# An encoder layer on one core: the sample's squares, the gating by feature, and layer norm's end on other engines

## The chip, the core and the metric

The kernel runs on one core of a Trainium2 chip. The core has five engines that run side by side, each taking its own instructions strictly in their order: TensorE (PE in the profile; its weight loads are listed apart as PEld), VectorE (DVE), ScalarE (ACT), GpSimd (POOL) and SyncE (SP), which here issues most of the DMA transfers. They wait for one another through semaphores. Matmul results land in PSUM, of which the program uses eight banks of 128 x 512 fp32; everything else lives in SBUF with 128 partitions. The metric is the device time of one execution in microseconds (us).

## What is computed

A bidirectional encoder layer with a final norm, on two groups of tokens that share all weights: `prompt` (1024 tokens) and `sample` (256 tokens), 1024 features, fp32. Cut to what matters here:

```
h = rmsnorm(x, norm_mix_w)                 # mean of squares over the 1024 features
proj = h @ w_in                            # columns split into:
#   qkv (1536), ab (16), dn_gate (512), sg_u (512), sg_v (512), gate_a, gate_b (1024 each)
y_a = deltanet_branch(qkv, ab, dn_gate, ...) @ w_up_a
u = gelu(sg_u);  v = layernorm(gelu(sg_v), ln_w, ln_b)       # over 512 columns
mixed = einsum('gts,bnsgc->bntgc', w_s, v in chunks of 128 tokens) + b_s
y_b = (u * mixed) @ w_up_b
x = x + (sigmoid(gate_a) * y_a + sigmoid(gate_b) * y_b) @ w_out
x = x + memory_cross_attention(rmsnorm(x), rmsnorm(mem, norm_mem_w), ...)
x = x + swiglu(rmsnorm(x)) ;  y = rmsnorm(x, final_norm_w)
```

The deltanet branch is a gated delta rule in both directions. The change touches only the start: the norms of x and mem, and the gating columns `sg_v` with `ab`.

## The kernel before

Activations lie with features on the partitions: a tile `xs` or `x` is 8 feature blocks of 128 (k = 0 to 7) by tokens. Tokens come in three blocks, b = 0 (prompt, 512), b = 1 (prompt, 512) and b = 2 (sample, 256), and the work starts with b = 2, then 0, then 1. Every matmul is done to full precision with three matmuls of a faster format: each operand is split into a rounded part `hi` (ACT, L125) and a rest `lo` (DVE or POOL, L126), and PE adds hi by hi, lo by hi and hi by lo.

The first norm (`first_norm`, L379) squares `xs` on ACT, two features at a time (128 x 512), adds the four squares on DVE (`nacc`, L250), and lets PE sum over the partitions by a matmul of each 128-token slice with a column of ones (`one`, part of the constants `cst`). DVE takes the mean and a reciprocal root by ten small steps (`rsqrt`, L225 to L229, result `nst`), PE spreads it over the partitions (`bank<-cst,nst`), and then each feature is scaled (DVE, `nt`, L285) and split into `hi` and `lo`. The squares and the scaled features share three buffers (`nsq`, `nt`). The norms of x0, x1 (blocks 0 and 1) and mem (the memory tokens) run in `other_norms` (L395) beside other work, with one feature of 512 tokens in each addition.

The gating (`sgv`, L513) has tokens on the output partitions: for each chunk of 128 tokens (2 in b = 2, 4 in the others) and each half of the columns (264 and 248 plus 16 for `ab`), 24 matmuls of 264 columns, 3 for each feature. The weights are `svh` and `svl`. The result goes through a gelu (ACT square, DVE, ACT tanh, DVE: L426 to L429) into `vg`. Then `ln` (L445) takes the layer norm of `vg`: squares on ACT (`junk`), `rsqrt` on DVE (`sums`), and `vg = (vg - mu) * rs` on DVE (L458). Between the blocks come the projections `sgu(g, b)` (L561), 24 matmuls with `whi` and `wlo`, whose gelu writes `ug`; later `mix` (L544) multiplies `vg` with the spatial weights on PE (`bank<-sw,vg`) and adds to `ug`. `decays` (L463) turns `ab` into the decays (`gm`) of the delta rule by some thirty DVE steps.

PSUM is two pools of four banks: `pm` for the long sums (gating, projections), `pq` for the short ones. A bank is handed out in turn, so a new sum waits until the readout of the fourth before it has ended. PE's order is the order in which the program is written: the main line (gating, projections) calls the side jobs (norms, `ln`, `mix`) whenever a planned clock, advanced by each matmul, passes the time that the side job asked for with `yield`. The other engines' instructions are ordered beside this by the scheduler.

## Time and profile before

| | us |
|---|---|
| three runs: median (lowest to highest) | 2224.17 (2222.96 to 2227.03) |
| the profiled execution | 2224.42 |
| its span from first to last instruction | 2222.6 |
| PE busy | 2179.2 |
| DVE, ACT, POOL busy | 1391.3, 866.9, 555.3 |
| mean granted clock of TensorE | 0.997 |

PE is busy for 98% of the span. The timeline lists instructions with start and duration; behind them in brackets stands how long the engine had been idle and what ended that (`<-`). Matmuls are pipelined and their ends are modelled: the next starts before one ends, so the pace is the difference of two starts. A 128 x 1 matmul in fp32 appears as two passes, each with its own weight load.

### The profile page before, as it was taken

To read this page: it belongs to the slowest core of one execution; us is meant where nothing else is said; L and a number is where in the kernel's file an instruction comes from. 1 tells how busy PE (TensorE), PEld (TensorE's weight loads), DVE (VectorE), ACT (ScalarE), POOL (GpSimd) and SP (SyncE) were. 2 spreads that over 40 slices of the span, in tenths; PEclk is the share of its full clock that TensorE was granted. 3 is DMA by queue.
4 is the path that set the end of the run, shared out by engine and by line. 5 is a ranking of instruction groups with operands and counts; after the bars stand their busy time and mean duration, and the time that the engine had idled before them with its cause. 6 is when DMAs were issued, how large, how long until landed. Compare 5 with 4: busy or idle time off the path is not lost.

```text
span 2222.6 us, 32341 instructions
## 1 busy us (share of the span) xinstructions
PE 2179.2 (98%) x12416; PEld 1906.1 (86%) x12416; DVE 1391.3 (63%) x2657; ACT 866.9 (39%) x1625; POOL 555.3 (25%) x358
## 2 busy tenths in 40 slices
PE   6999999999999999999999999999999999999998
PEld 5988889898988899888888888888888888888888
DVE  7767777786974864687654546734443444378575
ACT  5434153443525443124544423422322232343453
POOL 3010000000000000034421332466666666200031
PEclk9999999999999999999999999999999999999999
DMA  5222332223234455971421441222222222493631
GB/s 181 82 82 74 100 77 89 75 72 97 74 112 127 154 148 167 332 236 39 166 86 57 158 152 57 95 86 82 87 81 76 78 86 90 141 347 127 204 109 58
DMA packets 192821, 263.52 MB, mean 119 GB/s; under 512 B 72394, under 2 KB 102682, under 8 KB 192666
## 3 DMA queue, kind: packets, MB, share of 16 engines
q1 hardware_dynamic: 172826, 232.34, 31.8%
q10 hardware_dynamic: 19840, 29.11, 3.6%
q8 instruction: 97, 1.59, 0.3%
q14 instruction: 58, 0.48, 0.1%
HBM read 183.24 MB, written 78.16 MB: 118 GB/s over the span
## 4 chain that ended last, share of the span: by engine, by line
PE 82%; DVE 6%; issue 5%; DMA 4%; ACT 1%; POOL 1%; SPq 0%; POOLq 0%; ACTq 0%; DVEq 0%
PE bank L108 81%; PE bank L121 1%; DMA tbd<-stage 1%; DMA braw<-gq 1%; DVE wlo L1232 0%; DVE xf L126 0%; DMA stage<-gtd 0%; DVE lo L126 0%; DVE x L1441 0%; DMA t<-sgd 0%; DMA gb<-tbd 0%; DMA r<-in_w_out 0%; DVE nacc L250 0%; DVE wlo L126 0%; DVE nt L285 0%
## 5 line engine op out<-in xcount | busy, mean ns | idle before, releaser
L108 PE MATMUL bank<-hi,whi 128*128 128x512 f32 (+1 forms) x1976 | 701.9, 355 | 0.0
L108 PE MATMUL bank<-hi,wlo 128*128 128x512 f32 (+1 forms) x1976 | 687.0, 348 | 0.0
L108 PE MATMUL bank<-lo,whi 128*128 128x512 f32 (+1 forms) x1976 | 686.8, 348 | 0.0
L108 PEld LDWEIGHTS bank<-hi,wlo 128*128 128x128 f32 x1976 | 373.6, 189 | 48.8
L108 PEld LDWEIGHTS bank<-hi,whi 128*128 128x128 f32 x1976 | 374.4, 189 | 43.8 <-issue 0.2
L108 PEld LDWEIGHTS bank<-lo,whi 128*128 128x128 f32 x1976 | 374.6, 190 | 43.4 <-issue 0.2
L125 ACT ACTIVATE whi<-raw 128x1024 fp32r<-128x1024 f32 (+1 forms) x136 | 137.0, 1010 | 258.3 <-PE bank L108 219.2
L126 POOL TENSOR_TENSOR wlo<-raw,whi 128x1024 fp32r<-128x1024 f32 x65 | 157.2, 2420 | 307.4 <-ACT whi L125 307.4
L108 PE MATMUL bank<-bhl,whi 128*128 128x512 f32 x408 | 125.9, 390 | 0.1
L126 DVE TENSOR_TENSOR wlo<-raw,whi 128x1024 fp32r<-128x1024 f32 (+1 forms) x71 | 81.7, 1151 | 66.0 <-ACT whi L125 65.6
L126 POOL TENSOR_TENSOR wlo<-x,whi 128x1024 fp32r<-128x1024 f32 x40 | 97.4, 2435 | 47.6 <-ACT whi L125 47.6
L2013 DVE TENSOR_TENSOR x<-x,bank 128x512 f32<-128x512 f32 x21 | 14.5, 688 | 125.5 <-ACT x L1808 125.5
L108 PEld LDWEIGHTS bank<-bhl,whi 128*128 128x128 f32 x408 | 76.5, 188 | 16.5 <-ACT whi L125 0.5
L615 DVE SCALAR_TENSOR_TENSOR acc<-craw,sm,acc 128x510 f32<-128x510 f32 (+1 forms) x96 | 72.9, 759 | 25.9 <-ACT acc L613 24.2
L1821 DVE SCALAR_TENSOR_TENSOR t<-t,x 128x512 f32<-128x512 f32 x42 | 64.2, 1530 | 28.4 <-ACT t L1820 28.4
L108 PE MATMUL bank<-bhl,wlo 128*128 128x512 f32 x204 | 79.7, 391 | 0.7 <-DVE wlo L126 0.5
L125 ACT ACTIVATE whi<-x 128x1024 fp32r<-128x1024 f32 (+1 forms) x48 | 49.0, 1025 | 79.9 <-PE bank L108 73.7
L250 DVE TENSOR_TENSOR nacc<-nacc,nsq 128x512 f32<-128x512 f32 (+1 forms) x68 | 58.0, 852 | 34.0 <-ACT nsq L249 32.8
L1830 DVE SCALAR_TENSOR_TENSOR t<-bank,t 128x512 f32<-128x512 f32 (+1 forms) x44 | 24.5, 558 | 82.5 <-PE bank L108 82.5
L108 PE MATMUL bank<-bhl,ahl 128*128 128x512 f32 x312 | 75.0, 395 | 0.0
L883 POOL COPY UT<-U 64x512 f32<-64x512 f32 x20 | 14.9, 752 | 238.8 <-PE bank L108 235.8
L982 ACT ACTIVATE gs<-bank 128x512 f32<-128x512 f32 (+1 forms) x60 | 31.1, 518 | 108.3 <-PE bank L108 102.9
(373 smaller groups left out, 4578.5 us busy)
## 6 DMA issues: line engine op xcount, KB each, us to landing
raw<-in_w_gu SPq DMA_DIRECT2D x44, 512.0 KB, 3.5
braw<-gq SPq DMA_DIRECT2D x14, 1024.0 KB, 7.2
raw<-in_w_g SPq DMA_DIRECT2D x20, 512.0 KB, 3.3
gq<-t SPq DMA_DIRECT2D x33, 256.0 KB, 2.0
gtd<-gs ACTq DMA_DIRECT2D x32, 256.0 KB, 2.2
w<-in_w_dn SPq DMA_DIRECT2D x8, 1024.0 KB, 12.4
raw<-in_w_qkv SPq DMA_DIRECT2D x12, 512.0 KB, 3.6
gq<-r SPq DMA_DIRECT2D x22, 256.0 KB, 2.1
```

The source lines that it names most:

```text
L108: self.nc.tensor.matmul(out, l, r, start=start, stop=stop, skip_group_check=more)
L121: self.nc.tensor.transpose(out, x, ident)
L125: self.last_hi = self.nc.scalar.activation(hi, src, AF.Copy).ins
L126: (eng or self.nc.vector).tensor_tensor(out=lo, in0=src, in1=f32(hi), op=ALU.subtract)
L250: (eng or V).tensor_tensor(out=self.acc, in0=self.acc, in1=sq, op=ALU.add)
L615: V.scalar_tensor_tensor(out=dst, in0=src, scalar=wj, in1=dst, op0=ALU.mult, op1=ALU.add)
L883: G.tensor_copy(Um[q, hs, :], U[d][q, hs, :])
L982: S.activation(t, ps, AF.Tanh, scale=0.5)
L1821: V.scalar_tensor_tensor(out=t, in0=t, scalar=1.0, in1=src, op0=ALU.add, op1=ALU.mult)
L1830: V.scalar_tensor_tensor(out=out, in0=u, scalar=sign, in1=t, op0=ALU.mult, op1=ALU.mult)
L2013: V.tensor_tensor(out=c22, in0=c22, in1=pe, op=ALU.add)
```

## The change

Four edits, all in the first 135 us or so of the program:

- The first norm's squares are no longer added on DVE. PE sums each of them with the column of ones as it comes (16 matmuls into 16 columns of one bank instead of 4 with accumulation), and DVE adds over the features with one reduction.
- The first half of the gating goes by feature instead of by chunk for b = 2 and b = 0: all chunks' banks are opened at once, and for each feature each chunk gets its three matmuls. In these blocks the second half takes its first two banks from the other pool.
- Layer norm's end moves from DVE to ACT, as `vg * rs + (-mu * rs)`, with one more small DVE step for the second term.
- The seven additions of squares of x1's and of mem's norm move from DVE to POOL, with later planned times for what follows them.

```diff
--- before.py
+++ after.py
@@ -300,10 +300,10 @@
         rsqrt(y, ms, sc)
         yield lag2
 
-    def norm(p, xk, n, wcol, sink, pace=1300, step=700, lag=1500):
+    def norm(p, xk, n, wcol, sink, pace=1300, step=700, lag=1500, eng=None):
         nm = Norm(p, n)
         for k in range(KT):
-            nm.add(xk(k))
+            nm.add(xk(k), eng)
             yield step
         yield from nm.rest(xk, wcol, sink, pace, lag=lag)
 
@@ -377,12 +377,28 @@
     x_h = act_tiles()
 
     def first_norm():
-
-        nm = Norm(xp, 512)
+        nm = Norm(xp, NS)
+        pc = bank()
         for k in range(0, KT, 2):
-            nm.add(xs[:, k : k + 2, :].rearrange("p k t -> p (k t)"))
-        nm.n = NS
-        yield from nm.rest(lambda k: xs[:, k, :], S_MIX, to_h(x_h, 2), 0, lag=0, halves=2)
+            sq = xp.tile([P, 512], F32, tag="nsq", name="nsq", bufs=3)
+            S.activation(sq, xs[:, k : k + 2, :].rearrange("p k t -> p (k t)"), AF.Square)
+            for i in range(2):
+                for c in range(2):
+                    mm(pc[:, 2 * (k + i) + c : 2 * (k + i) + c + 1], sq[:, i * NS + c * P : i * NS + c * P + P], one)
+        y = xp.tile([P, 4], F32, tag="nst", name="nst", bufs=2)[:, :2]
+        ms, sc = pc[:, 16:18], pc[:, 18:20]
+        V.tensor_reduce(out=ms, in_=pc[:, :16].rearrange("p (k c) -> p c k", c=2), axis=AX.X, op=ALU.add)
+        V.tensor_scalar(out=ms, in0=ms, scalar1=1.0 / D, scalar2=EPS, op0=ALU.mult, op1=ALU.add)
+        rsqrt(y, ms, sc)
+        pb = bank()
+        for c in range(2):
+            mm(pb[:, c * P : (c + 1) * P], y[:, c : c + 1].to_broadcast([P, P]), ident)
+        sink = to_h(x_h, 2)
+        for k in range(KT):
+            t = xp.tile([P, 512], F32, tag="nsq", name="nt", bufs=3)[:, :NS]
+            V.scalar_tensor_tensor(out=t, in0=xs[:, k, :], scalar=sm[:, S_MIX + k : S_MIX + k + 1], in1=pb[:, :NS], op0=ALU.mult, op1=ALU.mult)
+            sink(k, t)
+            yield 0
 
     first = K.side(first_norm())
     sv_split(0, sv_raw0)
@@ -397,11 +413,11 @@
         done.add(0)
         x1_ = x_load(a["xT"], 512, 512, "x1")
         yield 3000
-        yield from norm(xp, lambda k: x1_[:, k, :], 512, S_MIX, to_h(x_h, 1), 900)
+        yield from norm(xp, lambda k: x1_[:, k, :], 512, S_MIX, to_h(x_h, 1), 900, lag=3000, eng=G)
         done.add(1)
         mem = x_load(a["memT"], 0, 512, "mem")
         yield 6000
-        yield from norm(xp, lambda k: mem[:, k, :], 512, S_MEM, lambda k, t: SY.dma_start(md[k], t))
+        yield from norm(xp, lambda k: mem[:, k, :], 512, S_MEM, lambda k, t: SY.dma_start(md[k], t), step=1400, lag=4000, eng=G)
 
     norms = K.side(other_norms())
 
@@ -454,8 +470,9 @@
         V.tensor_scalar(out=var[:, cs], in0=var[:, cs], scalar1=1.0 / 512, scalar2=4.0 * EPS, op0=ALU.mult, op1=ALU.add)
         yield 2000
         rsqrt(rs[:, cs], var[:, cs], s0[:, cs])
+        V.scalar_tensor_tensor(out=mu[:, cs], in0=mu[:, cs], scalar=-1.0, in1=rs[:, cs], op0=ALU.mult, op1=ALU.mult)
         for c in range(cs.start, cs.stop):
-            V.tensor_scalar(out=vg[:, c, :], in0=vg[:, c, :], scalar1=mu[:, c : c + 1], scalar2=rs[:, c : c + 1], op0=ALU.subtract, op1=ALU.mult)
+            S.activation(vg[:, c, :], vg[:, c, :], AF.Identity, scale=rs[:, c : c + 1], bias=mu[:, c : c + 1])
 
     lns = {}
 
@@ -513,24 +530,37 @@
     def sgv(b):
         if b < 2:
             K.until(norms, lambda: b in done)
+        hi, lo = x_h[b]
+        chunks = [(c, slice((c % 4) * P, (c % 4 + 1) * P)) for c in range(4 * b, min(4 * b + 4, NCH))]
+
+        def part(ps, half, cs, k):
+            wh, wl = wk(sv[half], k, 264)
+            for n, (l, r) in enumerate(((hi[:, k, cs], wh), (lo[:, k, cs], wh), (hi[:, k, cs], wl))):
+                mm(ps[:, :264], l, r, k == 0 and n == 0, k == KT - 1 and n == 2)
+
+        def readout(ps, half, c):
+            nv = 264 if half == 0 else 248
+            acc = (s0 if half == 0 else s1)[:, c : c + 1]
+            gelu2(sp, ps[:, :nv], vg[:, c, half * 264 : half * 264 + nv], nv, acc)
+            if half:
+                V.tensor_copy(ab[:, c, :], ps[:, 248:264])
+
         for half in (0, 1):
-            w = sv[half]
-            nv = 264 if half == 0 else 248
-            for c in range(4 * b, min(4 * b + 4, NCH)):
-                cs = slice((c % 4) * P, (c % 4 + 1) * P)
-                hi, lo = x_h[b]
-                ps = bank(pm)
-                n = 0
+            if half == 0 and b != 1:
+                pss = [bank(pm) for _ in chunks]
                 for k in range(KT):
-                    wh, wl = wk(w, k, 264)
-                    for l, r in ((hi[:, k, cs], wh), (lo[:, k, cs], wh), (hi[:, k, cs], wl)):
-                        mm(ps[:, :264], l, r, n == 0, n == 23)
-                        n += 1
+                    for ps, (c, cs) in zip(pss, chunks):
+                        part(ps, 0, cs, k)
+                        yield 0
+                for ps, (c, cs) in zip(pss, chunks):
+                    readout(ps, 0, c)
+                continue
+            for i, (c, cs) in enumerate(chunks):
+                ps = bank() if half and b != 1 and i < 2 else bank(pm)
+                for k in range(KT):
+                    part(ps, half, cs, k)
                     yield 0
-                acc = (s0 if half == 0 else s1)[:, c : c + 1]
-                gelu2(sp, ps[:, :nv], vg[:, c, half * 264 : half * 264 + nv], nv, acc)
-                if half:
-                    V.tensor_copy(ab[:, c, :], ps[:, 248:264])
+                readout(ps, half, c)
         lns[b] = K.side(ln(slice(4 * b, min(4 * b + 4, NCH))))
         K.ahead()
```

The order moves at three places that matter here. Behind a row stands, in brackets, whose semaphores it waits for (`Activation` is ACT, `Pool` POOL, `DMAHW` a transfer). First, ACT's queue at the split of the weights of the gating's second half (`svh_119`; `hi2_101` are the sample's features, `nsq` the squares of `x0`). Before:

```order
L125 ACTIVATE hi2_101<-nt_183 128x256 [waits DVE_49]
L249 ACTIVATE nsq_218<-x0_109 128x512 [waits Pool_49]
L249 ACTIVATE nsq_221<-x0_109 128x512 [waits DMAHW2_49,DVE_49]
L249 ACTIVATE nsq_224<-x0_109 128x512 [waits DVE_49]
L249 ACTIVATE nsq_227<-x0_109 128x512 [waits DMAHW3_49,DVE_49]
L249 ACTIVATE nsq_230<-x0_109 128x512 [waits DVE_49]
L125 ACTIVATE svh_119<-raw_114 128x1056 [waits DMAHW5_49]
```

After:

```order
L125 ACTIVATE hi2_101<-nt_190 128x256 [waits DVE_49]
L249 ACTIVATE nsq_230<-x0_109 128x512 [waits DVE_49,PE_49,Pool_49]
L125 ACTIVATE hi2_101<-nt_194 128x256 [waits DVE_49]
L249 ACTIVATE nsq_233<-x0_109 128x512 [waits DMAHW2_49,Pool_49]
L249 ACTIVATE nsq_236<-x0_109 128x512 [waits DVE_49]
L249 ACTIVATE nsq_239<-x0_109 128x512 [waits DMAHW3_49,DVE_49]
L125 ACTIVATE svh_119<-raw_114 128x1056 [waits DMAHW5_49]
```

One square now stands in front of the last `hi2`, and three instead of five between it and `svh_119`.

Second, PE at the gating of b = 0, first half (`bank_519` is one chunk's bank; `bank_531` to `bank_534` are the four chunks' banks; `hi0`, `lo0` the features). Before:

```order
L108 MATMUL bank_519<-svh_104,hi0_97 128x264 [waits PE_49,Activation_49]
L108 MATMUL bank_519<-svh_104,lo0_98 128x264 [waits Pool_49]
L108 MATMUL bank_519<-svl_103,hi0_97 128x264
L108 MATMUL bank_519<-svh_104,hi0_97 128x264 [waits Activation_49]
L108 MATMUL bank_519<-svh_104,lo0_98 128x264 [waits DVE_49]
L108 MATMUL bank_519<-svl_103,hi0_97 128x264
L108 MATMUL bank_519<-svh_104,hi0_97 128x264 [waits Activation_49]
L108 MATMUL bank_519<-svh_104,lo0_98 128x264 [waits Pool_49]
L108 MATMUL bank_519<-svl_103,hi0_97 128x264
L108 MATMUL bank_519<-svh_104,hi0_97 128x264 [waits Activation_49]
```

After:

```order
L108 MATMUL bank_531<-svh_104,hi0_97 128x264 [waits Activation_49]
L108 MATMUL bank_531<-svh_104,lo0_98 128x264 [waits Pool_49]
L108 MATMUL bank_531<-svl_103,hi0_97 128x264
L108 MATMUL bank_532<-svh_104,hi0_97 128x264
L108 MATMUL bank_532<-svh_104,lo0_98 128x264
L108 MATMUL bank_532<-svl_103,hi0_97 128x264
L108 MATMUL bank_533<-svh_104,hi0_97 128x264 [waits DVE_49]
L108 MATMUL bank_533<-svh_104,lo0_98 128x264
L108 MATMUL bank_533<-svl_103,hi0_97 128x264
L108 MATMUL bank_534<-svh_104,hi0_97 128x264 [waits DVE_49]
L108 MATMUL bank_534<-svh_104,lo0_98 128x264
L108 MATMUL bank_534<-svl_103,hi0_97 128x264
```

and on DVE after, the last feature's `lo0` and the gelu of `sgu(1,2)`, which reads `bank_466`, the bank that `bank_534` takes over (`bank_533` takes over that of `sgu(0,2)`):

```order
L227 SCALAR_TENSOR_TENSOR sums_215<-sums_215 128x2 [waits DVE_49]
L443 SCALAR_TENSOR_TENSOR gt_521<-gt_521,bank_466 128x256
L228 TENSOR_TENSOR sums_215<-sums_215 128x2 [waits DVE_49]
L229 SCALAR_TENSOR_TENSOR sums_215<-sums_215 128x2 [waits DVE_49]
L126 TENSOR_TENSOR lo0_98<-nt_513,hi0_97 128x512 [waits Activation_49]
L227 SCALAR_TENSOR_TENSOR sums_215<-sums_215 128x2 [waits DVE_49]
L445 SCALAR_TENSOR_TENSOR ug_520<-gt_521,bank_466 128x256 [waits Activation_49]
```

The first chunk went through all features before the next began; now the third and fourth chunk of the first feature wait for DVE, and PE has no further wait for a `lo0` that DVE writes.

Third, ACT around the squares of mem and, now, layer norm's end for b = 0 (`vg_214`; `gt` are the gelu steps). Before:

```order
L246 ACTIVATE nacc_941<-mem_873 128x512 [waits DMAHW5_49]
L249 ACTIVATE nsq_949<-mem_873 128x512 [waits Pool_49]
L428 ACTIVATE gt_917<-gt_917 128x512 [waits DVE_49]
L249 ACTIVATE nsq_968<-mem_873 128x512 [waits DMAHW6_49,Pool_49]
L249 ACTIVATE nsq_980<-mem_873 128x512
L249 ACTIVATE nsq_998<-mem_873 128x512 [waits DMAHW7_49,DVE_49]
L249 ACTIVATE nsq_1016<-mem_873 128x512 [waits DVE_49]
L426 ACTIVATE gt_953<-bank_922 128x512 [waits PE_49]
L249 ACTIVATE nsq_1028<-mem_873 128x512 [waits DMAHW0_49,DVE_49]
L249 ACTIVATE nsq_1046<-mem_873 128x512 [waits DVE_49]
L428 ACTIVATE gt_953<-gt_953 128x512 [waits DVE_49]
```

After:

```order
L246 ACTIVATE nacc_970<-mem_906 128x512 [waits DMAHW5_49]
L249 ACTIVATE nsq_987<-mem_906 128x512 [waits Pool_49]
L444 ACTIVATE gt_930<-gt_930 128x512 [waits DVE_49]
L249 ACTIVATE nsq_1005<-mem_906 128x512 [waits DMAHW6_49,Pool_49]
L249 ACTIVATE nsq_1029<-mem_906 128x512
L442 ACTIVATE gt_961<-bank_935 128x512 [waits PE_49,Activation_49]
L475 ACTIVATE vg_214<-vg_214,sums_215 128x512 [waits DVE_49]
L475 ACTIVATE vg_214<-vg_214,sums_215 128x512 x2
L475 ACTIVATE vg_214<-vg_214,sums_215 128x512 [waits Activation_49]
L444 ACTIVATE gt_961<-gt_961 128x512 [waits DVE_49]
L249 ACTIVATE nsq_1053<-mem_906 128x512 [waits DMAHW7_49,Pool_49]
```

The last passes over `vg` now stand in this queue, with mem's `nsq_1053` and a tanh behind them, and the squares wait for POOL where they waited for DVE.

## Prediction

> **What bounds the kernel now.** I read the page first, then busy time by stretch, then the instruction timeline of each engine over the first 135 us, since the order of the two programs differs nowhere behind that on the engines that TensorE (PE) waits for. The page says which engine is full, and the stretches say where it isn't (columns of the second view: stretch, its length, then busy us and instructions of PE, PEld, DVE, ACT and POOL, the granted clock, DMA share and GB/s).

> ```profile
> span 2222.6 us, 32341 instructions
> PE 2179.2 (98%) x12416; PEld 1906.1 (86%) x12416; DVE 1391.3 (63%) x2657; ACT 866.9 (39%) x1625; POOL 555.3 (25%) x358
> ```

> ```profile
> 0.00:20.00 20.00, 7.13 (x27) 6.14 (x28) 10.06 (x27) 9.31 (x16) 5.12 (x9) 1.00 0.88 311
> 20.00:52.00 32.00, 25.63 (x174) 23.22 (x174) 27.82 (x68) 18.57 (x37) 14.10 (x8) 0.94 0.25 75
> 52.00:102.00 50.00, 50.00 (x362) 47.88 (x361) 39.95 (x119) 27.28 (x58) 5.53 (x4) 0.97 0.27 98
> 102.00:135.00 33.00, 31.25 (x200) 27.73 (x199) 26.51 (x80) 12.08 (x28) 4.96 (x2) 1.00 0.27 98
> 135.00:2222.00 2087.00, 2065.15 (x11661) 1801.11 (x11659) 1286.92 (x2365) 799.65 (x1488) 525.55 (x336) 1.00 0.36 118
> ```

> PE is the bound. Of its 43.4 idle us, 12.9 lie in the first 20, 6.4 from 20 to 52, none from 52 to 102 and 1.8 up to 135. Behind 135 all keeps its order, so the change is worth what it does to PE's arrival there. So a gain has at most 21 us to come from, and much of that is the loading of the inputs.

> **1. Sample's squares on TensorE.** The timeline of the first norm (start, duration, engine, line, output and inputs, idle time before it and what ended it):

> ```profile
> 2.75 0.47 SPq L373 DMA_DIRECT2D sm<-in_small  x1
> 3.26 0.43 SPq L374 DMA_DIRECT2D cst<-in_const  x1
> 7.37 0.17 DVE L421 TENSOR_SCALAR h<-sm 128x9 f32<-128x9 f32 x1 [1.75 <-DMA sm<-in_small]
> 7.46 1.49 DVE L250 TENSOR_TENSOR nacc<-nacc,nsq 128x512 f32<-128x512 f32 x2
> 9.00 1.78 PEld L108 LDWEIGHTS bank<-cst,nacc 128*128 128x128 f32 x8 [9.00 <-DVE nacc L250]
> 9.00 1.87 PE L108 MATMUL bank<-cst,nacc 128*128 128x1 f32 x8 [9.00 <-DVE nacc L250]
> 13.11 1.22 PE L108 MATMUL bank<-cst,nst 128*128 128x128 f32 x4 [2.24 <-DVE nst L229]
> 31.61 0.95 PE L108 MATMUL bank<-cst,nacc 128*128 128x1 f32 x8
> ```

> The three additions on DVE go (they end at 8.95). In their place stand 16 column sums instead of 4. In the trace four such instructions are eight passes, 1.78/8 = 0.22 us each at 9.00; the same eight take 0.95 us at 31.61, where PE has warmed up. The sums need the column of ones. Its load is issued behind `sm`, and `sm` is awaited until 7.37, so PE starts no sooner than about 7.5, whenever the squares are there. 32 passes at 0.22 end at 7.5 + 7.1 + 0.1 = 14.7, where DVE took the result at 10.9 before: 3.8 later. The added reduction over features I put at 0.2, by the small DVE instruction at 7.37 (0.17). Together **+4.0**. At the warm price (0.12 a pass) the same sum is 7.5 + 3.8 + 0.2 = 11.5, +0.6. I take the cold one: it is the same work at the same place, and there PE had idled before it as it will again. DVE's rsqrt, PE's spread at 13.11 and the eight features only move along. The fourth square now waits for PE to free a buffer (9.4 instead of 6.5). Behind it on ACT stands the split of the gating weights; PE needs these with the first feature, which is itself 4 us later, so this costs nothing.

> [...]

> **2. What the second half of the gating waits for.** This norm is not what PE waits for longest:

> ```profile
> 20.44 2.82 ACT L249 ACTIVATE nsq<-x 128x512 f32<-128x512 f32 x5 [0.18 <-POOL lo L126]
> 23.17 1.07 ACT L125 ACTIVATE svh<-raw 128x1056 fp32r<-128x1056 f32 x1
> 24.31 2.94 POOL L126 TENSOR_TENSOR svl<-raw,svh 128x1056 fp32r<-128x1056 f32 x1 [3.90 <-ACT svh L125]
> 24.87 0.28 PE L108 MATMUL bank<-svh,lo 128*128 128x264 f32 x1
> 27.31 0.40 PE L108 MATMUL bank<-svl,hi 128*128 128x264 f32 x1 [2.17 <-POOL svl L126]
> ```

> PE finishes the sample's first half just before 24.87 and then waits 2.17 for `svl`, that is for ACT, which squared five features of x0 ahead of `svh`. So a faster first half is worth nothing here: by feature, PE does both chunks while the features come, and waits longer at the same place. Cost and gain of that edit at b = 2: 0, covered by this wait. What moves is ACT's queue. Three squares now stand between the last `hi` and `svh`, and one has slipped in front of the last `hi`. One square less is 2.82/5 = 0.56; at best the two that are gone and the pause after the last `hi` count in full, 1.4. I take **-1.1**. It goes against the +4.0, because all eight `hi` stand ahead of `svh`: PE starts the second half 2.9 later than at 27.31, and x0's norm behind it as well.

> **3. By feature at b = 0.** Here the four chunks open four banks at once, and the pool has four. Two of them are still held by the projections `sgu(0,2)` and `sgu(1,2)`, and the order shows PE waiting for DVE at the third and fourth chunk of the first feature, with DVE's release of the last one behind all eight `lo`.

> ```profile
> 50.57 0.69 DVE L126 TENSOR_TENSOR lo<-nt,hi 128x512 fp32r<-128x512 f32 x1
> 51.25 0.41 DVE L429 SCALAR_TENSOR_TENSOR ug<-gt,bank 128x256 f32<-128x256 f32 x1
> 44.09 0.29 PE L108 MATMUL bank<-svh,hi 128*128 128x264 f32 x1
> 51.32 0.49 PE L108 MATMUL bank<-svh,lo 128*128 128x264 f32 x1 [0.34 <-DVE lo L126]
> 54.24 0.42 PE L108 MATMUL bank<-svl,hi 128*128 128x264 f32 x1
> 54.46 0.42 PE L108 MATMUL bank<-svh,hi 128*128 128x264 f32 x1
> 62.83 0.28 PE L108 MATMUL bank<-svh,hi 128*128 128x264 f32 x1
> 62.95 0.28 PE L108 MATMUL bank<-svh,lo 128*128 128x264 f32 x1
> ```

> The last `lo` is the first row, the release (the write of `ug`) the second: 51.66. Before, PE had by then done the whole first chunk, 24 of 96 matmuls, between the features. Now it has done 9 of them, from 44.09 on, and has 87 left instead of 72 or 73: 14.5 more at 0.12 (62.83 to 62.95), **+1.75**. The slow stretch remains: after 51.32 matmuls follow at 0.22 (54.24 to 54.46), and PE will have been idler still. One slow stretch of this length more or less is 1.6 us, so this term lies between +0.1 and +3.4. Using the other pool for two chunks of the second half hides the four readouts that now come together: PE has two chunks, 5.8 us, before it needs a bank of theirs.

> **4. x1's and mem's sums on GpSimd, layer norm's end on ScalarE.** Rows from the groups (the POOL row) and from the timeline:

> ```profile
> L250 POOL TENSOR_TENSOR nacc<-nacc,nsq 128x512 f32<-128x512 f32 x14 | 22.3, 1595 | 164.6 <-ACT nsq L249 163.7
> 84.83 2.34 ACT L249 ACTIVATE nsq<-mem 128x512 f32<-128x512 f32 x4
> 88.69 1.92 DVE L458 TENSOR_SCALAR vg<-vg,sums 128x512 f32<-128x512 f32 x4
> 89.71 1.44 PE L108 MATMUL bank<-sw,vg 128*128 128x128 f32 x8
> 121.70 2.43 POOL L126 TENSOR_TENSOR wlo<-raw,whi 128x1024 fp32r<-128x1024 f32 x1 [42.08 <-ACT whi L125]
> 121.80 2.35 DVE L228 TENSOR_TENSOR sums<-sums 128x4 f32<-128x4 f32 x1
> 127.06 3.95 DVE L458 TENSOR_SCALAR vg<-vg,sums 128x512 f32<-128x512 f32 x4
> ```

> POOL does such an addition in 1.6 us, so each norm's seven take 11.2. For x1 that is hidden: they run beside the 87 matmuls, and PE asks for the sum 30 matmuls after those. For mem the seven additions are done long before PE asks, too. But ACT's squares of mem, POOL's additions and the small DVE steps of layer norm's rsqrt for b = 0 now meet in one place, and PE stands behind them: the mix `sw,vg` at 89.71. Before, `vg` was ready from 88.69 on, in 1.92 us, and PE hardly waited. Now x1's spread stands 13 matmuls later, so its features and with them layer norm's squares come 13 x 0.12 = 1.6 later. Four additions of mem that stood among DVE's steps are off DVE, which is worth up to 2.8 and, as DVE paused among them, about 1.9. One step more is added (0.2), and four passes on ACT take 2.34 (four squares of the same size) instead of 1.92. Undisturbed: 1.6 - 1.9 + 0.2 + 0.4 = +0.3.

> The disturbance is the pair at 121.7: a DVE step on 4 columns took 2.35 because POOL was at work. Three additions can meet DVE's steps (the fourth square waits behind `vg` on ACT). None gives +0.3, all three 0.3 + 4.8 = 5.1. I take one, 0.3 + 1.6 = **+1.9**. Behind `vg` on ACT wait the tanh of the open readout and mem's later squares, for which PE has slack.

> **5. The same for b = 1.**

> ```profile
> 104.38 2.06 DVE L285 SCALAR_TENSOR_TENSOR nt<-mem,sm,bank 128x512 f32<-128x512 f32 x3 [0.46 <-issue]
> 125.44 0.44 DVE L497 SCALAR_TENSOR_TENSOR gm<-wk,rows 128x32 f32<-128x32 f32 x4
> 127.78 0.63 PE L108 MATMUL bank<-cst,gm 128*40 128x128 f32 x4
> ```

> mem's spread comes some 70 matmuls later, so five of its eight passes (2.06/3 = 0.69 each, 3.4 in all) now stand between the last readout and the decays `gm`. PE took `gm` 1.9 after DVE had it, so 1.5 of this shows. Against it, `vg` leaves DVE, where it took 3.95 beside POOL: on ACT 2.34, 1.6 less. Net **0**, from -1.6 (the passes find room) to +3 (POOL's weight splits hit the decays).

> Sum: 4.0 - 1.1 + 1.75 + 1.9 + 0 = +6.6. The profiled execution took 2224.42 for its span of 2222.6; its own time plus 6.6 is **2231.0**. The median of the runs shown, 2224.17, is 0.25 lower, well inside their spread of 4.

> **The rivals.** [...]

> *By feature pays at b = 0* (not slower). If the banks were free in time, before PE reaches the third chunk six matmuls after 44.09, all 96 matmuls would run from 44.09 without a gap: 11.5 + 0.75 for the mixes between, done at 56.4 instead of 62.83. That is -6.5 in place of +1.75, in all 2222.8, or 2218 with the better ends of the other terms. It decides at the release of `ug`: before about 45 it pays, and in the trace the last came at 51.66. Against it stands the order on DVE; I see nothing for it but the possibility that I misread which bank is reused.

> *GpSimd's additions meet everything.* All three at b = 0 (+3.2 on my term) and the weight splits at b = 1 (+3): 2237. For it stand the rows at 121.7 and 127.06.

> **How the numbers follow.** Forecast 0.48 (2231, own range 2226 to 2235), warm sums 0.25 (2228.4), by feature 0.15 (2222.8), additions meet everything 0.12 (2237). A measurement of this kernel tells about 0.2% (4.4 us) from no change, so faster is below 2219.8, slower above 2228.6. Slower: 0.36 of the forecast's 0.48, 0.12 of the second, all 0.12 of the last: 0.60. Faster: 0.08 of the third, 0.02 of the first and 0.01 of the second: 0.11. The rest, 0.29, is the same. The range 2220 to 2237 leaves out about 0.1 below and 0.07 above.

> **What would show it.** Right: the rsqrt of the first norm starts on DVE near 15, the second half of the gating near 30; at b = 0 PE makes nine matmuls on the first feature, with two waits on `ug`, and stands until some 54; the first mix of b = 0 has a wait of about 2 us on ACT. Wrong: the first column sum before 7.3 or passes at 0.12 from the start; no wait on `ug`; DVE's small steps at 0.2 while GpSimd adds. If PE is at 135 us' place within 4 us of before, terms 3 and 4 were too dear.

## Result and the profile after

The changed kernel takes 2238.45 us (median of four runs, 2237.0 to 2241.14) against 2223.57 (2222.61 to 2227.03) for the kernel before on the same chip: a ratio of 1.0067, 95% interval 1.0055 to 1.008. It is slower by about 15 us; the forecast was slower by 6.6. The direction held and most of the waits stand where they were expected; the size did not hold, and one term of the sum, the decays of b = 1, was reckoned wrongly. The traced execution of the changed kernel is the fastest of its four, at 2237.0.

The page after, first lines, and busy time by stretch (columns as in the prediction):

```profile
span 2235.2 us, 32397 instructions
PE 2188.2 (98%) x12440; PEld 1916.3 (86%) x12440; DVE 1377.9 (62%) x2634; ACT 873.5 (39%) x1635; POOL 574.5 (26%) x372
```

```profile
0.00:20.00 20.00, 9.13 (x38) 8.47 (x39) 5.41 (x19) 7.57 (x11) 3.71 (x7) 1.00 0.82 278
20.00:52.00 32.00, 24.27 (x170) 22.36 (x169) 28.62 (x69) 19.98 (x41) 15.26 (x10) 0.98 0.27 92
52.00:102.00 50.00, 45.33 (x294) 42.39 (x295) 30.37 (x85) 28.51 (x59) 19.62 (x16) 0.91 0.26 90
102.00:135.00 33.00, 33.00 (x235) 31.16 (x234) 20.73 (x72) 11.47 (x29) 6.37 (x4) 1.00 0.23 84
135.00:160.00 25.00, 21.43 (x97) 17.60 (x96) 13.12 (x35) 7.54 (x12) 2.34 (x1) 0.80 0.19 66
```

The last stretch in the kernel before:

```profile
135.00:160.00 25.00, 25.00 (x139) 21.70 (x138) 10.91 (x19) 5.61 (x10) 2.52 (x5) 1.00 0.20 72
```

Before, PE was never idle from 52 to 102; now it stands 4.7 us there, and 3.6 us more from 135 to 160. In both stretches the granted clock is down as well (0.91 and 0.80). These two columns together are most of the result: PE waits, and then works at half speed. The 1.00 of the first stretch is no proof of a full clock: the first clock record of this trace comes at 23.67 us, and the column reads 1.00 ahead of it. What shows the half clock there is the pace, 0.22 us a pass.

How late PE is can be read from one and the same matmul in both timelines. Its start before and after, and what was lost since the row above:

| matmul | before | after | late | lost here |
|---|---|---|---|---|
| spread of the first norm | 13.11 | 16.58 | +3.47 | +3.5 |
| second half of b = 2, first with `svl` | 27.31 | 29.17 | +1.86 | -1.6 |
| first of the gating of b = 0 | 44.09 | 45.32 | +1.23 | -0.6 |
| first of `sgu(0,0)`, behind it | 76.29 | 80.66 | +4.37 | +3.1 |
| first of `sgu(0,1)`, behind the gating of b = 1 | 115.01 | 124.27 | +9.26 | +4.9 |
| behind the third mix of b = 0 | 147.97 | 163.34 | +15.37 | +6.1 |
| 2207 us, near the end | | | +12.86 | -2.5 |

PE's timeline after, at these places:

```profile
7.17 6.96 PE L108 MATMUL bank<-cst,nsq 128*128 128x1 f32 x32 [7.17 <-DMA cst<-in_const]
16.58 1.22 PE L108 MATMUL bank<-cst,nst 128*128 128x128 f32 x4 [2.46 <-DVE nst L229]
29.17 0.39 PE L108 MATMUL bank<-svl,hi 128*128 128x264 f32 x1 [1.53 <-POOL svl L126]
48.80 0.39 PE L108 MATMUL bank<-svh,hi 128*128 128x264 f32 x1 [2.59 <-DVE ug L445]
53.00 0.59 PE L108 MATMUL bank<-svh,hi 128*128 128x264 f32 x1 [3.57 <-DVE ug L445]
80.66 0.40 PE L108 MATMUL bank<-hi,whi 128*128 128x512 f32 x1
97.15 0.49 PE L108 MATMUL bank<-sw,vg 128*128 128x128 f32 x2 [2.91 <-ACT vg L475]
97.85 0.49 PE L108 MATMUL bank<-sw,vg 128*128 128x128 f32 x2 [0.22 <-ACT vg L475]
98.56 1.50 PE L108 MATMUL bank<-sw,vg 128*128 128x128 f32 x4 [0.22 <-ACT vg L475]
139.87 1.08 PE L108 MATMUL bank<-cst,gm 128*40 128x128 f32 x4 [2.76 <-DVE gm L514]
141.76 2.91 PE L108 MATMUL bank<-sw,vg 128*128 128x128 f32 x8 [0.81 <-ACT vg L475]
```

The waits are where the prediction put them: two on `ug`, one on `vg`, one on the decays `gm`. Behind the long ones stands a stretch at half clock. The first mix of b = 1 is no measure of it: its passes come two by two, 0.70 us apart, which is the pace at which ACT writes `vg`, and they do so in e5 below as well, where the clock is 1.00. The granted clock behind the wait on `vg` and behind that on `gm`, of the kernel after:

```profile
97.00:103.00 6.00, 5.35 (x26) 4.68 (x27) 2.47 (x4) 5.44 (x11) 2.42 (x2) 0.72 0.00 1
139.00:150.00 11.00, 9.32 (x30) 7.28 (x31) 5.58 (x18) 4.25 (x7) 0.62 (x1) 0.53 0.22 75
```

0.72 over 6 us is one stretch of some 3.4 us at half, 0.53 over 11 us is nearly all of it.

What the waits at b = 0 and b = 1 come from stands on DVE (one ACT row among them): the small steps of the layer norm of b = 0 that met GpSimd's additions, `vg`, and at b = 1 the first and last of mem's five late passes, two small steps that met GpSimd's weight split, and the decays.

```profile
91.93 1.21 DVE L228 TENSOR_TENSOR sums<-sums 128x4 f32<-128x4 f32 x1
93.37 1.14 DVE L227 SCALAR_TENSOR_TENSOR sums<-sums 128x4 f32<-128x4 f32 x1
95.03 0.82 DVE L228 TENSOR_TENSOR sums<-sums 128x4 f32<-128x4 f32 x1
96.28 2.93 ACT L475 ACTIVATE vg<-vg,sums 128x512 f32<-128x512 f32 x4 [2.49 <-DVE sums L473]
126.25 0.73 DVE L285 SCALAR_TENSOR_TENSOR nt<-mem,sm,bank 128x512 f32<-128x512 f32 x1
...
130.57 0.74 DVE L285 SCALAR_TENSOR_TENSOR nt<-mem,sm,bank 128x512 f32<-128x512 f32 x1
131.22 2.35 DVE L504 TENSOR_TENSOR wk<-wk 128x80 f32<-128x80 f32 x1
...
137.32 2.32 DVE L228 TENSOR_TENSOR sums<-sums 128x4 f32<-128x4 f32 x1
139.56 0.43 DVE L514 SCALAR_TENSOR_TENSOR gm<-wk,rows 128x32 f32<-128x32 f32 x4
```

From the last `ab` copy to `gm` DVE took 8.4 us before (117.08 to 125.44) and takes 13.2 now (126.33 to 139.56).

### The profile page after: what moved, and what is told of

Read it like the earlier page. It is cut to its first block, busy times and chain, and to the rows that moved or that the text cites. A ratio compares the mean times of both kernels' runs of the same rounds, so it can differ in the third digit from the quotient of the medians.

```text
span 2235.2 us, 32397 instructions
## 1 busy us (share of the span) xinstructions
PE 2188.2 (98%) x12440; PEld 1916.3 (86%) x12440; DVE 1377.9 (62%) x2634; ACT 873.5 (39%) x1635; POOL 574.5 (26%) x372
## 4 chain that ended last, share of the span: by engine, by line
PE 82%; DVE 7%; issue 4%; DMA 4%; ACT 2%; POOL 1%; SPq 0%; POOLq 0%; DVEq 0%; ACTq 0%
PE bank L108 81%; DMA tbd<-stage 1%; PE bank L121 1%; DVE xf L126 1%; DMA braw<-gq 1%; DVE x L1471 1%; DVE nt L285 1%; DMA t<-sgd 1%; DVE wlo L1262 1%; DVE lo L126 0%; DMA stage<-gtd 0%; DVE wlo L126 0%; DMA gb<-grd 0%; DMA raw<-in_w_u 0%; POOL nacc L250 0%
## 5 line engine op out<-in xcount | busy, mean ns | idle before, releaser
L108 PE MATMUL bank<-hi,whi 128*128 128x512 f32 (+1 forms) x1976 | 703.4, 356 | 0.0
L108 PE MATMUL bank<-hi,wlo 128*128 128x512 f32 (+1 forms) x1976 | 688.2, 348 | 0.3 <-POOL wlo L126 0.3
L108 PE MATMUL bank<-lo,whi 128*128 128x512 f32 (+1 forms) x1976 | 688.0, 348 | 0.0
L108 PEld LDWEIGHTS bank<-hi,wlo 128*128 128x128 f32 x1976 | 374.4, 189 | 49.5 <-POOL wlo L126 0.5
L108 PEld LDWEIGHTS bank<-hi,whi 128*128 128x128 f32 x1976 | 375.5, 190 | 44.1 <-issue 0.2
L108 PEld LDWEIGHTS bank<-lo,whi 128*128 128x128 f32 x1976 | 375.7, 190 | 43.7 <-issue 0.2
L125 ACT ACTIVATE whi<-raw 128x1024 fp32r<-128x1024 f32 (+1 forms) x136 | 137.0, 1010 | 257.3 <-PE bank L108 218.1
L126 POOL TENSOR_TENSOR wlo<-raw,whi 128x1024 fp32r<-128x1024 f32 x65 | 157.7, 2428 | 295.7 <-ACT whi L125 295.7
L108 PE MATMUL bank<-bhl,whi 128*128 128x512 f32 x408 | 125.9, 390 | 0.0
L126 DVE TENSOR_TENSOR wlo<-raw,whi 128x1024 fp32r<-128x1024 f32 (+1 forms) x71 | 81.6, 1150 | 66.6 <-ACT whi L125 66.4
L126 POOL TENSOR_TENSOR wlo<-x,whi 128x1024 fp32r<-128x1024 f32 x40 | 97.5, 2437 | 46.9 <-ACT whi L125 46.8
L108 PEld LDWEIGHTS bank<-bhl,whi 128*128 128x128 f32 x408 | 76.4, 188 | 16.5 <-ACT whi L125 0.5
L250 POOL TENSOR_TENSOR nacc<-nacc,nsq 128x512 f32<-128x512 f32 x28 | 40.7, 1455 | 180.9 <-ACT nsq L249 179.2
L125 ACT ACTIVATE whi<-x 128x1024 fp32r<-128x1024 f32 (+1 forms) x48 | 49.0, 1025 | 79.9 <-PE bank L108 73.7
L108 PE MATMUL bank<-bhl,wlo 128*128 128x512 f32 x204 | 79.6, 390 | 0.5 <-DVE wlo L126 0.5
L913 POOL COPY UT<-U 64x512 f32<-64x512 f32 x20 | 14.9, 752 | 238.0 <-PE bank L108 235.0
L108 PE MATMUL bank<-bhl,ahl 128*128 128x512 f32 x312 | 75.0, 395 | 0.0
```

The lines of the kernel that those rows point to most:

```text
L108: self.nc.tensor.matmul(out, l, r, start=start, stop=stop, skip_group_check=more)
L125: self.last_hi = self.nc.scalar.activation(hi, src, AF.Copy).ins
L126: (eng or self.nc.vector).tensor_tensor(out=lo, in0=src, in1=f32(hi), op=ALU.subtract)
L250: (eng or V).tensor_tensor(out=self.acc, in0=self.acc, in1=sq, op=ALU.add)
L913: G.tensor_copy(Um[q, hs, :], U[d][q, hs, :])
```

## Experiments

e1 to e10 take the change apart; v1 and v2 try to make the kernel before faster. "Late" is, as above, how much later than in the trace of before PE starts the same matmul; these differences come from one profiled execution of each kernel, and between two executions they scatter by a microsecond or two. The last column is the difference of the medians, each against runs of the kernel before that were timed beside it. These were four groups (the change; e1 to e4; e5 to e8; e9, e10, v1 and v2), so a difference between two rows of different groups carries the scatter of both.

| kernel | at 44.09 | at 76.29 | at 115.01 | at 147.97 | near the end | medians |
|---|---|---|---|---|---|---|
| the change | +1.23 | +4.37 | +9.26 | +15.37 | +12.86 | +14.9 |
| e1 squares on PE alone | +1.43 | +1.78 | +1.79 | +1.78 | +1.32 | +1.6 |
| e2 by feature alone | -0.38 | +2.30 | +2.29 | +3.58 | +6.30 | +7.6 |
| e3 layer norm's end alone | -1.41 | -1.08 | +0.68 | +1.90 | +1.79 | +2.6 |
| e4 sums on GpSimd alone | -1.68 | -1.26 | +6.89 | +11.22 | +10.16 | +13.1 |
| e5 change, PE kept busy | +1.61 | +3.96 | +7.61 | +11.85 | +8.97 | +10.5 |
| e6 change, sums on DVE | +2.20 | +4.57 | +10.97 | +16.00 | +14.89 | +13.1 |
| e7 change, old planned times | +1.74 | +4.77 | +7.05 | +6.79 | +5.50 | +4.8 |
| e8 change, free banks | +1.69 | +1.41 | +6.43 | +12.57 | +12.59 | +11.3 |
| e9 change, mem's old times | +2.01 | +4.48 | +8.92 | +8.70 | +4.13 | +8.9 |
| e10 squares on PE, warmed | +0.11 | +0.01 | +0.04 | +0.04 | -2.41 | +0.1 |
| v1 by feature, free banks, alone | -0.47 | -5.23 | -3.05 | -3.05 | -0.14 | +0.4 |
| v2 before, PE kept busy | -0.22 | +0.65 | +0.67 | +2.21 | -0.26 | -1.0 |

### Each edit alone

Alone the four edits cost 1.6, 7.6, 2.6 and 13.1, which is 24.9 together, against 14.9 for the change: they are not independent, and what one costs depends on the others.

e1 has the new `first_norm` only, e2 the new `sgv` only, e3 the new end of `ln` only:

```diff
 # e4: the kernel before with
-            nm.add(xk(k))
+            nm.add(xk(k), eng)
...
-        yield from norm(xp, lambda k: x1_[:, k, :], 512, S_MIX, to_h(x_h, 1), 900)
+        yield from norm(xp, lambda k: x1_[:, k, :], 512, S_MIX, to_h(x_h, 1), 900, lag=3000, eng=G)
...
-        yield from norm(xp, lambda k: mem[:, k, :], 512, S_MEM, lambda k, t: SY.dma_start(md[k], t))
+        yield from norm(xp, lambda k: mem[:, k, :], 512, S_MEM, lambda k, t: SY.dma_start(md[k], t), step=1400, lag=4000, eng=G)
```

> Edit 1 alone: only the first norm's squares go to TensorE, all else as before. Theory (costs are local: each edit costs what PE waits at its own place, plus a stretch at half clock where the wait is long): PE's spread of the first norm at 16.6 us instead of 13.1, the second half of the gating near 29.2 instead of 27.3, the first matmul of b = 0 near 45.3 instead of 44.1, and no more behind it: about +1 us in all. Rival (the parts only hurt together: a shift at the start throws later engines out of step): +4 us or more, with new waits of PE behind 80 us.

> Edit 2 alone: the first half of the gating by feature for b = 2 and b = 0. Theory: nothing at b = 2; at b = 0 two waits on ug in the first feature, the second one until about 52 us, then cold matmuls to about 57; the first projection matmul behind b = 0's gating about 3 us later than at 76.29 and no other loss: +3 us in all. Rival (the banks' release is only late because the first norm was late): the waits are shorter than 2 us together, 0 or below.

> Edit 3 alone: layer norm's end on ScalarE, the sums of squares stay on DVE. Theory (the long wait at b = 0 is the lateness of the layer norm's small steps, not ACT): the mix of b = 0 waits less than 0.5 us for vg; at b = 1 the wait of 1.32 for vg shrinks, since the four passes no longer run on DVE beside GpSimd: -1 to 0 us in all. Rival (ACT is the cause, as the wait's name in the trace says: its passes take 0.73 us each instead of 0.48 and stand in a queue): a wait of over 2 us at the first mix of b = 0 and a half-clock stretch behind it, +4 us or more.

> Edit 4 alone: x1's and mem's sums on GpSimd with the later planned times. Theory: the layer norm's small steps at b = 0 meet three additions, vg comes 2 to 3 us after PE asks, then a half-clock stretch: +4; at b = 1 the five passes of mem and the weight split stand ahead of the decays, PE waits 2 to 3 us for gm and runs at half clock behind it: +4 to +6. Together +8 to +10 us, most of what the whole change costs. Rival (ACT is the cause): +2 to +4, from b = 1 alone.

e1: 2225.01 against 2223.37, ratio 1.0005 (0.9996 to 1.0014). The spread of the first norm starts at 16.69, all is 1.8 late at 76.29 and stays so to 148 us. As the theory had it.

e2: 2230.95, 1.0034 (1.0022 to 1.0047). The two waits on `ug` (2.53 and 3.58) are there without any of the other edits, so the banks are late by themselves, and the gating of b = 0 loses 2.7 (-0.38 to +2.30). The rest of its +6.3 was lost in a half-clock stretch at 133 us and further on, above all between 900 and 960 us (+4.0 to +5.9) and in a half-clock stretch near 1257 us (+5.4 to +7.0), where PE's order is that of before; the expected +3 was the right size for the place and too little for the whole.

e3: 2225.93, 1.0008 (0.9998 to 1.0018). PE's view at b = 0:

```profile
89.22 0.49 PE L108 MATMUL bank<-sw,vg 128*128 128x128 f32 x2 [0.44 <-ACT vg L459]
89.93 0.49 PE L108 MATMUL bank<-sw,vg 128*128 128x128 f32 x2 [0.22 <-ACT vg L459]
```

The first wait is under 0.5 as expected, and the rival's wait of over 2 us is not there. But each of the four passes over `vg` comes 0.71 after the one before, and PE waits for each, where before it took the whole mix in 1.2 us (89.71 to 90.91): +1.8 at this stage that the theory had not counted.

e4: 2236.43, 1.006 (1.0047 to 1.0073): nearly the whole loss, and more than the theory's +8 to +10. DVE and PE at b = 0:

```profile
90.44 5.60 DVE L458 TENSOR_SCALAR vg<-vg,sums 128x512 f32<-128x512 f32 x4
```

```profile
91.87 0.49 PE L108 MATMUL bank<-sw,vg 128*128 128x128 f32 x2 [3.26 <-DVE vg L458]
93.29 0.49 PE L108 MATMUL bank<-sw,vg 128*128 128x128 f32 x2 [0.92 <-DVE vg L458]
94.69 0.80 PE L108 MATMUL bank<-sw,vg 128*128 128x128 f32 x2 [0.92 <-DVE vg L458]
```

The four passes over `vg`, 1.92 us before, take 5.60 beside GpSimd's additions: 1.40 each, the time of one addition. So the third edit is in part a remedy for the fourth. Alone the two cost 1.8 and 8.2 at this stage (76.29 to 115.01); in the change, which has the other two edits as well, the stage loses 4.9. The trace shows one DVE pass per addition (the additions start 1.35 to 1.41 apart there); what holds the pass back it does not show.

### Contention or planned time?

e6 takes `eng=G` out of the change, e7 takes `lag` and `step` out, e9 takes out mem's `step` and `lag` only:

```diff
 # e7: the changed kernel with
-..., 900, lag=3000, eng=G)
+..., 900, eng=G)
...
-..., step=1400, lag=4000, eng=G)
+..., eng=G)
```

> The changed kernel with x1's and mem's additions back on DVE, at the changed kernel's planned times. Theory (the later place of x1's and mem's spreads makes the layer norm and the decays late; GpSimd's additions add little over the DVE additions that they replace): the first mix of b = 0 still waits about 2 us, the decays still wait 2.8 us with five of mem's passes ahead of them: -1 to -3 us against the changed kernel. Rival (GpSimd's additions, which stretch three small steps by 2.7 us, are the cause): no wait and no half-clock stretch at b = 0, -5 us or more.

> The changed kernel with the additions on GpSimd, but x1's and mem's planned times as before the change. Theory (times): x1's spread comes 1.9 us earlier, so the first mix of b = 0 waits about 1 us and the clock holds; mem's passes are done before the decays, whose wait goes: -3.5 and -6. Against it mem's sum, now asked for at about 103 us, is not ready before some 107, since four of its squares stand behind vg on ACT: +4 and a half-clock stretch. In all -3 to -5. Rival (GpSimd's additions): the wait at b = 0 stays at 2.5 to 3 us, and the gain is that of b = 1 less the new wait, 0 to -2.

> The changed kernel with only mem's planned times as before the change; x1's keep the later one, and all additions stay on GpSimd. Theory (each norm's later time costs at one place, x1's at the first mix of b = 0, mem's at the decays of b = 1): the first mix of b = 0 still waits about 2.9 us and runs at half clock behind it, the decays' wait of 2.76, vg's of 0.81 and the half clock from 140 us on are gone: about -6 us against the changed kernel. Rival (mem's squares and additions also make the layer norm of b = 0 late): the wait at b = 0 falls below 1.5 us as well, -8 to -10 us.

First mix of b = 0 in e6, then first mix and decays in e7 and in e9:

```profile
97.90 2.21 PE L108 MATMUL bank<-sw,vg 128*128 128x128 f32 x6 [3.46 <-ACT vg L475]
```

```profile
95.62 0.49 PE L108 MATMUL bank<-sw,vg 128*128 128x128 f32 x2 [0.97 <-ACT vg L475]
...
134.83 0.63 PE L108 MATMUL bank<-cst,gm 128*40 128x128 f32 x4
```

```profile
96.98 0.49 PE L108 MATMUL bank<-sw,vg 128*128 128x128 f32 x2 [2.63 <-ACT vg L475]
...
136.70 0.63 PE L108 MATMUL bank<-cst,gm 128*40 128x128 f32 x4
```

e6: 2237.64 against 2224.57, 1.0059 (1.0047 to 1.0072). With no addition on GpSimd the wait at b = 0 is longer, not shorter. DVE's own additions stand among the same small steps and stretch the chain as much: from 90.47 to 96.26, 5.8 us, against 6.0 in the change. ACT then starts on `vg` only at 97.05, behind two squares of mem. The rival falls.

e7: 2229.38, 1.0022 (1.0011 to 1.0033), the only one of these that takes most of the loss away, about 10 us. The small steps meet GpSimd four times there (7.0 us in all), and still PE waits only 0.97, since they begin 2.5 us earlier. At b = 1 there is no wait for `gm` at all and nothing is lost (+7.05 to +6.79). The wait for mem's sum that was expected to eat 4 us of this did not come.

e9: 2232.87 against 2223.96, 1.004 (1.0027 to 1.0052). b = 0 loses nearly what it loses in the change (4.4 of 4.9), b = 1 nothing. Its trace is of the fastest of its five executions, 2228.81, so the +4.13 near the end is less than its median shows. So x1's later time costs at b = 0, mem's at b = 1, each at one place. The planned times, which say where in PE's order the column sums and spreads stand and, for mem, how far apart its squares are added, are the main loss of the change; on which engine the sums are added matters little, as long as `vg` is not on DVE beside them (e4). Which of mem's two numbers, `lag` or `step`, does it was not separated, and the new times without the other edits were not run.

### The clock

e5 fills the waits of the change with idle matmuls:

```diff
         pmx = bank()
+        if g == 0 and b < 2:
+            fill(pmx, 22 if b == 0 else 6)
...
         pr = bank()
+        fill(pr, 22)
...
+    def fill(ps, n):
+        for _ in range(n):
+            T.matmul(ps[:, :264], x_h[0][0][:, 0, :P], sv[0][0][:, :264], start=True, stop=True)
```

> The changed kernel with 22, 22 and 6 idle matmuls (128 x 264, into a bank that the next real sum overwrites) ahead of the first mix of b = 0, of the decays' matmul and of the first mix of b = 1, so that TensorE works where it waited 2.91, 2.76 and 0.81 us. Theory (the half-clock stretches behind these places come from TensorE's standing still): 22 matmuls take 2.6 us and fit into the waits, the matmuls behind them run at 0.12 instead of 0.22, the stretches of 3.4 us near 99 and 10 us from 140 go: -1.7 and -3.3, about -5 us in all. Rival (the waits alone are the cost, the clock falls for another reason): no change, or as much slower as the fillers overrun the waits, 0 to +1.

```profile
96.79 0.49 PE L108 MATMUL bank<-sw,vg 128*128 128x128 f32 x2 [0.32 <-ACT vg L475]
...
138.27 0.63 PE L108 MATMUL bank<-cst,gm 128*40 128x128 f32 x4 [0.16 <-DVE gm L518]
...
140.16 0.49 PE L108 MATMUL bank<-sw,vg 128*128 128x128 f32 x2 [0.33 <-ACT vg L475]
```

```profile
135.00:160.00 25.00, 23.13 (x139) 19.70 (x139) 12.21 (x29) 8.53 (x14) 4.00 (x2) 1.00 0.14 50
```

2235.08 against 2224.57, 1.0048 (1.0035 to 1.006): 4.4 less than the change. The real work starts no earlier: the first mix of b = 0 comes 16.5 us behind the first matmul of `sgu(0,0)` in both, the decays' matmul 15.6 behind that of `sgu(0,1)`. But the clock reads 1.00 from 135 to 160 where it read 0.80, and the two stages lose 3.7 and 4.2 instead of 4.9 and 6.1. So about 3 us of the loss up to 148 us was half clock and nothing else (5 were expected), and it goes when PE does not stand still.

e10 puts three idle matmuls ahead of the column sums of e1:

```diff
-        nm = Norm(xp, NS)
+        nm = Norm(xp, 512)
         pc = bank()
+        V.memset(nm.acc, 1.0)
+        for w in (512, 512, 256):
+            T.matmul(pc[:, :w], nm.acc[:, :P], nm.acc[:, :w], start=True, stop=True)
```

> Edit 1 alone, with three idle matmuls of 128 x 512, 512 and 256 on a constant tile ahead of the first column sum, while TensorE waits for the inputs. Theory (the column sums ran at 0.22 a pass because one-column passes do not raise the clock; wide ones do): the idle matmuls take some 5 us from about 1 us on, the 32 passes behind them run at 0.12 where the squares are there, the spread of the first norm comes at 13 to 14 us instead of 16.7, the second half of the gating at about 27: -2 us against edit 1 alone, -1 to 0 against the kernel before. Rival (the clock is slow in the first 15 us whatever TensorE does): passes of 0.22 as in edit 1 alone, spread at 16.7, no gain.

PE's first instructions, and PE by microsecond (busy us, passes, granted clock, DMA share, GB/s):

```profile
1.45 4.63 PE L384 MATMUL bank<-nacc 128*128 128x512 f32 x6 [1.45 <-DVE nacc L382]
7.70 4.69 PE L108 MATMUL bank<-cst,nsq 128*128 128x1 f32 x32 [1.61 <-DMA cst<-in_const]
```

```profile
9.00:10.00 1.00, 1.00 (x11) 1.00 0.98 364
10.00:11.00 1.00, 1.00 (x8) 0.60 1.02 365
11.00:12.00 1.00, 1.00 (x6) 0.50 1.03 362
```

2224.10 against 2223.96, ratio 1.0 (0.9992 to 1.0009); e1 alone was at 1.0005, with overlapping intervals, so the gain is seen in the trace only: the spread comes at 14.85 instead of 16.69. Behind the wide matmuls the column sums run at 11 passes a microsecond. But after some 2.5 us of them, with PE busy throughout, the clock falls to half (0.60 from 10 to 11 us, 0.50 from 11 to 12), and 6 passes a microsecond are left, as in the change. Whether the pause of 1.6 us ahead of them has its part in that was not separated: the clock was at full from 6.78 to 10.19, and 0.9 us of the pause lie in that stretch. In the change, 6.96 us of such passes without a pause stayed at 0.22 us a pass. Both sides were partly right: the start is not slow by itself, but the one-column passes did not keep the clock up here.

### Free banks, and what is late next

```diff
 # e8: the changed kernel with
-                pss = [bank(pm) for _ in chunks]
+                pss = [bank(pm) if i < 2 else bank() for i in range(len(chunks))]
...
-                ps = bank() if half and b != 1 and i < 2 else bank(pm)
+                ps = bank() if half and b == 2 and i < 2 else bank(pm)
 # v1: the kernel before with this sgv, and
-        yield MIX
+        yield MIX + (6000 if b == 2 and g < 2 else 0)
 # and x1's lag 5500, mem's load 3000 and its lag 1000 earlier
```

> The changed kernel with two of the four banks of b = 0's first half from the other pool, so that none is held by the projections. Theory (the two waits on ug are the loss of the edit by feature): no wait on ug, TensorE follows the features and ends the first half 6 to 8 us earlier; next late is x1's sum on GpSimd, which ends at about 66 us, so 3 to 4 us of that stay: -3 to -6 in all. Rival (TensorE is bound by the features' arrival there whatever the banks): less than -1.

> The kernel before with edit 2 alone, but with free banks: at b = 0 two of the four banks come from the other pool, the two mixes of b = 2 that stood in this half are planned 6 us later, x1's sum 4 us later (so that its additions on DVE are done) and mem's 4 us earlier. Theory (TensorE loses nothing but the banks' waits by the new order): the first half of b = 0 ends 6 us earlier, near 57 instead of 62.8; 2 to 3 us of it are lost at b = 0's first mix, where the layer norm is next late: -3 to -4 us against the kernel before. Rival (layer norm and decays, which hang on DVE, set the pace of this part whatever TensorE does): all of it is waited for again by 150 us, 0 to +3.

First mix of b = 2 in e8, first mix of b = 0 in v1:

```profile
55.38 1.50 PE L108 MATMUL bank<-sw,vg 128*128 128x128 f32 x4 [3.64 <-ACT vg L475]
```

```profile
85.76 1.40 PE L108 MATMUL bank<-sw,vg 128*128 128x128 f32 x6 [1.12 <-DVE vg L458]
```

e8: 2235.91 against 2224.57, 1.0051 (1.0039 to 1.0064), 3.5 less than the change. No wait on `ug` is left and the stage loses nothing (+1.69 to +1.41). Next late is not x1's sum, as expected, but the layer norm of b = 2, whose mix stands in this half.

v1: 2224.31 against 2223.96, 1.0001 (0.9992 to 1.001). With that mix moved away, PE is 5.2 us ahead at 76.29: the edit by feature can do what it seems made for. Of this 2.2 go between the gating of b = 0 and that of b = 1, where PE waits 1.12 for `vg` and 0.83 for mem's sum, and the rest melts behind 900 us. In the end it is no faster. PE's arrival at 135 us is not all that sets the end, then: between 900 and 960 us, where the change gave back 1.8 us, PE stands still for 4.2 us in this trace and for 2.6 in that of before, and there alone the lateness changes by up to 1.9 us, up in some kernels and down in others. Besides, nine of the fourteen traces, v1's and the change's among them but not that of before, have one half-clock stretch of 3.41 us between 1249 and 1269 us, and lose 1.2 to 1.5 us from 1200 to 1300; the other four kernels of the table lose nothing there. PE's order at both places is that of before. What decides either stays open; so up to 3 us of a difference near the end cannot be put down to an edit from one trace.

### Filling the waits of the kernel before

```diff
+                warm = half == 0 and c == 0
+                fb = bank() if warm else None
...
+                    for _ in range(3 if warm and k < 7 else 0):
+                        T.matmul(fb[:, :264], hi[:, k, cs], wh, start=True, stop=True)
```

> The kernel before with three idle matmuls of 128 x 264 behind each of the first seven features of b = 0's first chunk, where TensorE waits for the features. Theory (the half clock behind this stretch, 51.4 to 54.8 us in the trace of before, comes from TensorE's standing still; the idle matmuls fit into the waits): no half-clock stretch there, the second chunk at 0.12 from the start, -1.7 us. Rival: the idle matmuls only delay the features' own, 0 to +1.

```profile
65.23 0.91 PE L108 MATMUL bank<-cst,nacc 128*128 128x1 f32 x7 [2.18 <-DVE nacc L250]
```

2222.96 against 2223.96, ratio given as 1.0001 (0.9992 to 1.0009; the quotient of these two medians would be 0.9996). The half-clock stretch at 51 to 55 us is gone and the first half of b = 0 ends earlier by 1.5 (-1.74 at 62.83, against -0.22 at 44.09), about as expected; and then PE waits 2.18 for x1's sum, which hangs on DVE's additions. No version here beats the kernel before clear of noise.

## Why the prediction was wrong in size

The step that failed is the fifth term, the decays of b = 1: it was put at 0 by setting a gain of `vg` against a loss of `gm`, although `gm` is what PE asks for first, and it measured +6.1. Next to it, the term for the layer norm of b = 0 priced a wait without the half clock behind it. The terms in order:

**First norm, +4.0.** Measured +3.5. All 32 passes ran cold, 6.96 us where the sum had 7.1, and the first started at 7.17, not 7.5. The rival with warm sums (0.25, 2228.4) needed part of these passes at 0.12; no run shows one-column passes that raise the clock. In the change all 32 stayed at 0.22, and in e10, where they began at 11 a microsecond, they fell to 6 after some 2.5 us.

**Second half of b = 2, -1.1.** Measured -1.6, by the mechanism named (`svh` 2.2 later, eight `hi` ahead of it). Another -0.6 up to 44.09 came unasked: in the trace of before the clock fell to half behind the 2.17 us wait there (0.50 from 27.56 to 30.97), in that of the change it did not fall behind 1.53 (see the last section).

**By feature at b = 0, +1.75 (0.1 to 3.4).** Measured +3.1. Mechanism as forecast to the matmul: nine on the first feature, two waits on `ug`, the second until 53.00 (54 forecast). The 14.5 matmuls were right. Half clock behind the last wait lasted 4.8 us (53.00 to 57.80) where it was 3.2 before, 0.8 of the 1.4 that remain; the rest was not located. The rival "by feature pays" had its condition unmet: PE got the last two banks at 48.80 and 53.00, not before 45. v1, with free banks and the mixes of b = 2 moved away, meets it, and PE then gains 4.8 at this stage, where the rival had 6.5.

**Layer norm of b = 0, +1.9 (0.3 to 5.1).** Measured +4.9, within the term's range. x1's spread came 1.8 later relative to PE, as worked out (1.6). Three steps met additions, not one, but an addition took 1.3 there, not 1.6, and each step lost the rest of one only, 2.7 in all. What failed here: a wait was priced as its length. It was 3.35 with the two short ones, and the half clock behind it (98.76 to 102.17) was some 1.5 more.

**Decays of b = 1, 0 (-1.6 to +3).** Measured +6.1: this is the term that broke the forecast. The wait itself was expected, 1.5 of it, and was 2.76. Five of mem's passes stood ahead of `gm`, just as said, at 0.65 to 0.74 each. But the 1.6 that `vg` gained by leaving DVE was set against it, and `vg` stands behind `gm` on PE: it was worth the 0.5 by which its own wait shrank. The second weight split, 2.3, which before came behind `gm`, now met a small step ahead of it. Both were rows of the trace of before. And nearly all of 139 to 150 us ran at half clock, for which the sum had nothing. e9 takes wait and half clock away by mem's times alone.

**The sum.** Terms of +6.6, measured +15.4 at 148 us. Of the 8.8 between, 6.1 are the decays, 3.0 the layer norm and 1.4 the gating; the first two terms were 1.6 too dear. The rival "additions meet everything" gave 2237, closest in number, for the wrong reason: e6 has no additions on GpSimd and is nearly as slow. That PE's arrival at 135 us sets the end, on which all the terms rest, held only roughly: the traced execution gave back 2.5 of its 15.4 on the way to the end.

## What to carry to other kernels

A number that only shifts a step in a planned order is an edit like any other: list what it is moved past on every engine, and who behind that is already just in time. Price a stall of TensorE as its length plus up to 1.7 us for each stretch of half clock that may follow: such a stretch lasted 3.41 us in these traces, and idle time from 0.97 us up went ahead of one at some places, while at another waits of up to 1.58 us did not. And an engine relieved of work is worth only what the first wait behind it shows, not the work's length.
